# Feed-forward stages with engine orders written by hand, and six inner tiles to a group in place of four

## The chip, the cores and the metric

The kernel runs on one NeuronCore of a Trainium2 chip. The time is device microseconds of one execution, as the runtime measures it; the number given for a kernel is the median of its runs. One execution was also recorded by the hardware profiler, and its span is counted from the first to the last instruction in that record.

Names of engines: PE is TensorE (matmuls), DVE is VectorE, ACT is ScalarE, POOL is GpSimd, SP is SyncE, which here only issues the transfers. PSUM is the memory that PE writes and DVE and ACT read, SBUF the working memory.

## The reference, cut to what matters

One decoder layer on 1024 tokens and 16 meta tokens in front of them (1040 columns in all), width 1024, inner width 2816. It is a feed-forward block, a mixing block with two kinds of attention, and a second feed-forward block:

```
def swiglu(x, w_gate, w_up, w_down):
    return (jax.nn.silu(x @ w_gate) * (x @ w_up)) @ w_down
...
h = h + 0.5 * swiglu(rmsnorm(h, norm_ffn1[l]), w_ffn1_gate[l], w_ffn1_up[l], w_ffn1_down[l])
...
h = h + merged @ w_out[l]
h = h + 0.5 * swiglu(rmsnorm(h, norm_ffn2[l]), w_ffn2_gate[l], w_ffn2_up[l], w_ffn2_down[l])
```

Everything is float32. The change touches the two feed-forward blocks alone; the first works on 1040 columns, the second on 1024.

## The kernel before, in words

**Numbers.** Each float32 operand is split into two float16 parts, a high one (written by ACT) and the rest, a low one (written by DVE, value minus high part). A product is then three matmuls: high by high, high by low, low by high.

**Tiles.** The 2816 inner channels are 22 inner tiles of 128. The columns are two halves (528 and 512 in the first block, 512 and 512 in the second). One *product* is a block of weights by a block of one column half: for a gate or an up projection four contraction tiles times three matmuls, in the first block twice that, since a half goes into two PSUM banks there (S = 2), and once in the second (S = 1).

**Seven products for eight.** Two inner tiles, two halves of the contraction and two halves of the columns make a two by two block product. `fast` does it with seven products in place of eight, named p1, p6, p7, p5, c11, p74 and p53. For that the weights of the pair are combined (`sums`: four additions on DVE), and the columns too (`combine`: four subtractions on POOL, once for the normed input in `make_t`, and once per pair of inner tiles for the hidden values). The products land in PSUM tiles pa, pb, pc and pd; p7 goes into pc, is taken out by DVE, and p74 later adds into the same pc; so p74 waits until DVE has taken p7 out. A set of seven products is called a *job* here: a gate job, an up job, or a down job (two output tiles d and d+1 for all inner tiles of a group).

**Stages of a block.** `plain_pair` does the first pair of inner tiles with eight products while `make_t` builds the combined columns; this is the head. Then pairs follow: an up job of the pair, the split of its hidden values (`split_x`, tile `hid`: three tiles, and four combined ones after POOL), and the gate job of the next pair. After each group of inner tiles (`F_GROUPS`) four down jobs add the group's share to `h`. The last group's down projection is plain: eight tiles d per column half, one PSUM tile `pdn` each.

**Weights.** `load_raw` brings 128x1024 float32 from memory by the SP queue into one of two `wst` buffers; `wide_weights` (gate and up) and `joint_weights` (down) make the split and combined weights of a job from one or two of them.

**Order.** Nothing fixes the order by hand: the tile framework's scheduler interleaves all instructions by its own estimates of time when the kernel is built, and each engine then runs its list in that order, waiting where a semaphore has not come.

Lines that the text speaks of (before): L320 matmuls of a job; L144 to L146 plain matmuls; L129 and L130 high and low part of weights; L325 to L328 sums of weights; L234 and L235 high and low part of `hid`; L282 to L285 `combine`; L386, L391, L393, L397, L401 DVE takes p6, p7, p5, p74, p53 of a gate or up job out of PSUM; L427 gate times up; L434 and L445 the same for a down job; L451 and L453 POOL adds a shared part of a down job to `h`; L503 takes `pdn` out; L218 and L221 norm the columns of the half that is done for the mixing block.

Of the kernel before, what the change touches and what calls it, by code (L numbers as in the profile page):

```python
# [26 lines left out]
TOPK = 256  # L27
NEG = -1e30
# [10 lines left out]
F_GROUPS = ((0, 4), (4, 8), (8, 12), (12, 16), (16, 22))  # L39
# [15 lines left out]
def layer_kernel(ctx: ExitStack, tc: tile.TileContext, xT, gains, wgu1, wd1, win, wvi, wbs, wbw, wout,  # L55
# [139 lines left out]
    def fpage(shape, dt, name):  # L195
        return ph["sb"].tile(shape, dt, tag="fp", name=name, bufs=22)
# [29 lines left out]
    def ffn(u, rb, hs, gi, wgu, wd, other_half, passes, saved):  # L226
# [10 lines left out]
        def new_hid(x):  # L237
            made[0] += 1
            return (fpage if made[0] <= 6 else hp)([P, 2, hs[x][0].shape[1]], F16, "hid")
# [18 lines left out]
        t_blocks, ahead = [], []  # L258

        def plain_pair(f):  # L260
            ws = [load_w(wgu[2 * f + i], 1024, raws.pop(0) if raws else None) for i in range(4)]
            vals = [None] * 4
            for x in range(2):
                if x == 1:
                    ahead.append(wide_weights(wgu[2 * f + 4], wgu[2 * f + 6]))
                    t_blocks.extend(make_t())
# [62 lines left out]

        def wide_weights(src1, src2):  # L330
# [4 lines left out]
            sa = ph["sb"].tile([P, 1024], F32, tag="wS", name="sa", bufs=2)  # L335
            sb = ph["sb"].tile([P, 1024], F32, tag="wS", name="sb", bufs=2)
# [4 lines left out]
            x3 = ph["sb"].tile([P, 2, 1024], F16, tag="ws", name="x3", bufs=2)  # L341
            split_w(x3, sb, 1024)
            x4 = ph["sb"].tile([P, 2, 512], F16, tag="w4", name="x4", bufs=2)
            split_w(x4, r2[:, hi], 512)
            return (x1, 0), (x1, 512), (x2, 0), (x2, 512), (x3, 0), (x3, 512), (x4, 0)

        def joint_weights(src, hn):
            r = load_raw(src, 4 * hn)
            q = [slice(i * hn, (i + 1) * hn) for i in range(4)]
            sa = ph["sb"].tile([P, 1024], F32, tag="wS", name="sa", bufs=2)  # L350
            sums(sa[:, q[2]], sa[:, q[0]], sa[:, q[1]], sa[:, q[3]], r[:, q[0]], r[:, q[1]], r[:, q[3]], r[:, q[2]])
            x1 = wsp_tile()
            split_w(x1, r, 3 * hn)
            x2 = wsp_tile()
            split_w(x2, sa, 4 * hn)
            return (x1, 0), (x1, hn), (x2, 0), (x2, hn), (x2, 2 * hn), (x2, 3 * hn), (x1, 2 * hn)

        def fast(weights, blocks):
            a11, a12, s2, s3, s1, s4, a22 = weights
            b11, b21, b22, t1, t2, t3, t4 = blocks  # L360
            pa, pb = wide("pa"), wide("pb")
            product(pa, *a11, b11, wa, wa, True, True)
            yield "p1", pa[:, :, :wa]
            product(pb, *s2, t2, wa, wa, True, True)
            yield "p6", pb[:, :, :wa]
            pc = wide("pc")
            product(pc, *s3, t3, wb, wb, True, True)
            yield "p7", pc[:, :, :wb]
            pd = wide("pd")
            product(pd, *s1, t1, wb, wb, True, True)  # L370
            yield "p5", pd[:, :, :wb]
            product(pa, *a12, b21, wa, wa, False, True)
            yield "c11", pa[:, :, :wa]
            product(pc, *a22, t4, wa, wa, False, True)
            yield "p74", pc[:, :, :wa]
            product(pd, *s4, b22, wb, wb, False, True)
            yield "p53", pd[:, :, :wb]

        def half_products(f, m, blocks, first, done, weights=None):
            make = fbtmp if m else ftmp  # L380
            for what, ps in fast(weights or wide_weights(wgu[2 * f + m], wgu[2 * f + 2 + m]), blocks):
# [22 lines left out]
        def gate_part(f, blocks, weights=None):  # L404
# [16 lines left out]
            half_products(f, 0, blocks, first, done, weights)  # L421
            return gates

        def up_part(f, blocks, gates):
# [31 lines left out]
        for g_, (f0, f1) in enumerate(F_GROUPS):  # L456
# [4 lines left out]
            for f in range(f0, f1, 2):  # L461
# [5 lines left out]
                if f == 0:  # L467
                    gates = gate_part(2, blocks, ahead.pop())
# [648 lines left out]
```

## Time and profile before

| | |
|---|---|
| runs | 2090.22, 2093.07, 2091.82 us, median 2091.82 |
| span of the profiled execution | 2087.6 us; the median of the runs lies 4.2 us above it |
| PE busy | 1953.8 us, 94% of the span |
| DVE busy | 1622.3 us, 78% |
| ACT, POOL busy | 906.1 us, 420.8 us |
| mean granted TensorE clock | 0.985 of 2.4 GHz |
| moved by DMA | 149.05 MB, mean 71 GB/s |
| first block, head / jobs / plain down | 0 to 111.7 / 111.7 to 648.7 / 648.7 to 716.2 us |
| mixing block | 716.2 to 1426.9 us |
| second block, head / jobs / plain down and end | 1426.9 to 1488.2 / 1488.2 to 2007.7 / 2007.7 to 2087.6 us |

How to read it: a matmul's record has a start that is measured and an end that is modelled, so two matmuls in a row overlap in the record, and 94% does not say that PE was at its peak for 94% of the time. What a matmul costs in a stream is read from start to start. A stretch of PE work is costed by counting its matmuls and multiplying by that step; what is left of the stretch was lost, to waits or to a lower clock.

### The profile page before, as it was taken

Reading aid. Unit: us, or ns where it says so; the run is one execution under the profiler, and the core shown is the slowest. Engines: PE = TensorE matmul, PEld = TensorE weight load, DVE = VectorE, ACT = ScalarE, POOL = GpSimd, SP = SyncE. Lnnn points to the kernel's source line nnn. Section 1 sums busy time; section 2 is a strip of 40 time slices with the busy share of each in tenths; the row PEclk is TensorE's granted clock in tenths of the full one; section 3 lists DMA queues with packets and bytes.
Section 4 is the critical chain, followed back from the end, with each engine's and each line's share of the span. In section 5 each row is a group of like instructions: output and inputs, shape, how many; then the busy total and the mean of one; then the engine's idle time right before and its main releaser. Section 6 shows DMA issues by size and latency. Waiting matters only on the chain.

```text
span 2087.6 us, 32850 instructions
## 1 busy us (share of the span) xinstructions
PE 1953.8 (94%) x13068; PEld 1198.1 (57%) x13068; DVE 1622.3 (78%) x2821; ACT 906.1 (43%) x1572; POOL 420.8 (20%) x329
## 2 busy tenths in 40 slices
PE   5899999989999999999999999998899989999997
PEld 4588887878888556554555654444344434444443
DVE  7978777686865789999999955657978686878755
ACT  4442333333333446589885643434433333332332
POOL 3613232231300123222001000003242231314000
PEclk9999999999999999999999999999999999999998
DMA  4021111111213543322010124241111121211223
GB/s 154 11 62 61 51 52 61 41 62 41 71 54 100 173 153 104 101 67 72 16 62 17 32 82 141 76 167 40 51 51 61 41 62 41 80 41 61 58 73 112
DMA packets 56569, 149.05 MB, mean 71 GB/s; under 512 B 7008, under 2 KB 13152, under 8 KB 56416
## 3 DMA queue, kind: packets, MB, share of 16 engines
q1 hardware_dynamic: 56416, 146.96, 22.0%
q8 instruction: 102, 1.67, 0.3%
q14 instruction: 51, 0.42, 0.1%
HBM read 132.11 MB, written 14.76 MB: 70 GB/s over the span
## 4 chain that ended last, share of the span: by engine, by line
PE 52%; DVE 30%; DMA 5%; issue 5%; ACT 4%; POOL 3%; DVEq 0%; SPq 0%; ACTq 0%; POOLq 0%
PE pc L320 10%; PE pd L320 9%; PE pa L320 8%; DVE wsp L130 5%; PE pb L320 4%; DMA wst<-in_wgu_dram 3%; DVE h L434 2%; PE p_br L914 2%; DVE x L130 2%; DVE hid L235 2%; PE pdn L146 2%; PE pdn L144 2%; PE pdn L145 2%; DVE u L221 2%; DVE sc L706 2%
## 5 line engine op out<-in xcount | busy, mean ns | idle before, releaser
L320 PEld LDWEIGHTS <-wsp 128*128 128x128 f16 x4896 | 480.2, 98 | 268.9 <-issue 33.6
L129 ACT ACTIVATE wsp<-wst 128x1024 f16<-128x1024 f32 (+2 forms) x200 | 185.4, 929 | 358.3 <-PE pc L320 197.5
L320 PEld LDWEIGHTS <-x 128*128 128x128 f16 x2160 | 215.2, 100 | 144.8 <-issue 42.8
L130 DVE SCALAR_TENSOR_TENSOR wsp<-wst,wsp 128x1024 f16<-128x1024 f32 (+2 forms) x200 | 242.2, 1212 | 66.1 <-ACT wsp L129 65.8
L320 PE MATMUL pa<-u,wsp 128*128 128x264 f16 (+1 forms) x1440 | 224.7, 310 | 0.0
L453 POOL TENSOR_TENSOR h<-h,base 128x512 f32<-128x512 f32 x64 | 117.7, 1838 | 219.0 <-DVE h L434 219.0
L146 PEld LDWEIGHTS <-wsp 128*128 128x128 f16 x992 | 97.8, 99 | 99.5 <-issue 12.3
L320 PE MATMUL pc<-tb,x 128*128 128x264 f16 (+1 forms) x720 | 122.9, 329 | 31.5 <-DVE c L391 31.5
L145 PEld LDWEIGHTS <-wsp 128*128 128x128 f16 x992 | 98.1, 99 | 88.2 <-issue 6.4
L144 PEld LDWEIGHTS <-wsp 128*128 128x128 f16 x992 | 98.4, 99 | 86.4 <-issue 4.0
L130 DVE SCALAR_TENSOR_TENSOR wsp<-sa,wsp 128x1024 f16<-128x1024 f32 x72 | 102.4, 1422 | 37.2 <-ACT wsp L129 37.2
L129 ACT ACTIVATE wsp<-sa 128x1024 f16<-128x1024 f32 x72 | 75.7, 1052 | 110.7 <-DVE sa L327 37.9
L320 PE MATMUL pb<-tb,wsp 128*128 128x264 f16 (+1 forms) x720 | 113.6, 311 | 9.2 <-ACT tb L234 5.6
L320 PE MATMUL pc<-tb,wsp 128*128 128x256 f16 (+1 forms) x720 | 114.2, 314 | 0.0
L320 PE MATMUL pd<-u,x 128*128 128x256 f16 (+1 forms) x720 | 111.0, 308 | 0.4
L320 PE MATMUL pd<-tb,x 128*128 128x256 f16 (+1 forms) x720 | 110.7, 308 | 0.0
L320 PE MATMUL pc<-hid,wsp 128*128 128x256 f16 (+2 forms) x576 | 94.4, 309 | 16.1 <-DVE h L434 15.9
L727 ACT ACTIVATE jk<-sc,s5nb 128x784 f16<-128x784 f32 (+2 forms) x93 | 97.8, 1052 | 19.0 <-DVE s5nb L742 15.3
L282 POOL TENSOR_TENSOR t<-g,g 128x512 f32<-128x512 f32 x14 | 22.9, 1634 | 376.6 <-DVE g L427 376.6
L146 PE MATMUL p_gate<-u,wsp 128*128 128x512 f16 x256 | 97.0, 379 | 1.4 <-DVE wsp L130 1.4
L144 PE MATMUL p_gate<-u,wsp 128*128 128x512 f16 x256 | 97.0, 379 | 0.0
L145 PE MATMUL p_gate<-u,wsp 128*128 128x512 f16 x256 | 97.0, 379 | 0.0
(223 smaller groups left out, 3986.3 us busy)
## 6 DMA issues: line engine op xcount, KB each, us to landing
wst<-in_wgu_dram SPq DMA_DIRECT2D x88, 512.0 KB, 3.5
wst<-in_win_dram SPq DMA_DIRECT2D x44, 512.0 KB, 3.5
wst<-in_wd_dram SPq DMA_DIRECT2D x32, 512.0 KB, 3.6
wst<-in_wd_dram SPq DMA_DIRECT2D x32, 384.0 KB, 3.2
wst<-in_wout_dram SPq DMA_DIRECT2D x16, 512.0 KB, 3.8
qscr<-ry SPq DMA_DIRECT2D x20, 256.0 KB, 2.2
q<-qscr SPq DMA_DIRECT2D x20, 256.0 KB, 3.1
wst<-in_wbs_dram SPq DMA_DIRECT2D x16, 256.0 KB, 2.9
```

What stands on the lines that cost most here:

```text
L129: nc.scalar.activation(sp[:, 0, :n], st[:, :n], AF.Copy, scale=WS)
L130: nc.vector.scalar_tensor_tensor(sp[:, 1, :n], st[:, :n], WS, sp[:, 0, :n], op0=ALU.mult, op1=ALU.subtract)
L144: nc.tensor.matmul(ps, w[:, 0, wcols], xt[:, 0, xcols], start=start, stop=False)
L145: nc.tensor.matmul(ps, w[:, 0, wcols], xt[:, 1, xcols], start=False, stop=False)
L146: nc.tensor.matmul(ps, w[:, 1, wcols], xt[:, 0, xcols], start=False, stop=stop)
L221: nc.vector.tensor_sub(u[k][:, 1, s0:s1], t[:, :w], u[k][:, 0, s0:s1])
L235: nc.vector.tensor_sub(dst[:, 1, :], src, dst[:, 0, :])
L320: nc.tensor.matmul(ps[:, s, :n], w[:, a, wc], tiles[k][:, y, s * stride:s * stride + n], start=start and k == 0 and j == 0, stop=stop and ...
L434: nc.vector.scalar_tensor_tensor(hv, ps, DS, hv, op0=ALU.mult, op1=ALU.add)
L453: nc.gpsimd.tensor_add(vb(hs[1][e]), vb(hs[1][e]), va(base)[:, :, :wb])
L706: nc.vector.match_replace(out=raw, in_to_replace=m8, in_values=raw, imm_value=MARK)
L727: nc.scalar.activation(junk[:, :w], sc[b][0], AF.Sign, bias=bias[:, j:j + 1], accum_out=s[:, j:j + 1])
```

## The change

It does the following, and nothing else:

- `F_GROUPS` has three groups of six inner tiles and a last one of four, where it had four of four and a last one of six. The order in which the down weights lie in memory follows it.
- All gate, up and down jobs of a block are listed beforehand (`jobs`). The raw weights of a job are fetched two jobs ahead (`fetch`) and prepared one job ahead (`prepare`), in 13 steps in a fixed order. `joint_weights` is gone: a down job now has two loads and four additions, each over all its inner tiles.
- Behind the matmuls of each product, `pump` writes out a seventh (by the weights that stand in the list) of the job's steps: those of the next job's weights and those that split the hidden values of the pair before. Then come the instructions that take the product out of PSUM.
- All this stands in a `manual_schedule` region for PE, DVE, ACT and POOL: on these four engines the order is that of the text. SP's order is still the scheduler's. The head (`plain_pair`) and the plain down projection stand outside.
- A down job does its products in the order p1, p7, p5, p6, c11, p74, p53, and one addition of POOL moves from p5 to p6.
- Buffers: 27 pages `fp` in place of 22; the hidden values of a group take up to 11 of these, 8 of `hp` and 2 of `nt`.

```diff
-F_GROUPS = ((0, 4), (4, 8), (8, 12), (12, 16), (16, 22))
+F_GROUPS = ((0, 6), (6, 12), (12, 18), (18, 22))
...
+        def fetch(i):
+            if i < len(jobs):
+                n = 2 * jobs[i][3]
+                fetched[i] = [load_raw(src, n) for src in jobs[i][1:3]]
...
+        def prepare(i):
...
+            r1, r2 = fetched.pop(i)
...
+            one, two = n / 750, n / 420
+            v = nc.vector
+            return [
+                (0, lambda: high(x1, r1, both)),
+                (one, lambda: v.tensor_add(sb[:, lo], r2[:, lo], r2[:, hi])),
+                (0, lambda: high(x4, r2[:, hi], n)),
+                (one, lambda: v.tensor_sub(sa[:, lo], sb[:, lo], r1[:, lo])),
+                (one, lambda: v.tensor_sub(sa[:, hi], r1[:, lo], r2[:, lo])),
+                (0, lambda: high(x2, sa, both)),
+                (one, lambda: v.tensor_sub(sb[:, hi], r1[:, hi], sa[:, lo])),
+                (two, lambda: low(x1, r1, both)),
+                (one, lambda: low(x4, r2[:, hi], n)),
+                (0, lambda: fetch(i + 1)),
+                (0, lambda: high(x3, sb, both)),
+                (two, lambda: low(x2, sa, both)),
+                (two, lambda: low(x3, sb, both)),
+            ]
...
+        def pump(t):
+            while todo and t > 0:
+                cost, step = todo.pop(0)
+                step()
+                t -= cost
...
+            share = sum(c for c, _ in todo) / len(order)
+            for name in order:
+                bank, w, tiles, stride, n, start = what[name]
+                if bank not in banks:
+                    banks[bank] = wide(bank)
+                ps = banks[bank]
+                product(ps, *w, tiles, stride, n, start, True)
+                pump(share)
+                yield name, ps[:, :, :n]
+            drain()
+
+        UP = ("p1", "p6", "p7", "p5", "c11", "p74", "p53")
+        DOWN = ("p1", "p7", "p5", "p6", "c11", "p74", "p53")
...
+            own = prepare(i + 1)
+            todo.extend(own[:7] + tail[:4] + own[7:10] + tail[4:] + own[10:])
...
+        vals = plain_pair(0)
+        blocks = (u[0][:4], u[0][4:], u[1][4:]) + tuple(t_blocks)
+        with tc.manual_schedule(engines=ORDERED):
+            for f0, f1 in F_GROUPS:
...
+                    if last:
+                        extra = []
+                        split_later(extra, vals[1], 1)
+                        hid += [[down[0][-1], extra[0]], [down[1][-1], down[2][-1]]]
+                        if f == NF - 2:
+                            drain()
...
+                if not last:
+                    for d in range(0, KD, 2):
+                        fast_down(d, down)
```

How the change moves instructions on DVE, at two places. First the passage from an up job to the gate job after it, in the first block: from the last product of the up job (gate times up, `g`) to where the gate job's p7 is taken out (`c<-pc,base`, L391 before, L458 now); `sa` and `sb` are sums of weights, `base<-pb` is p6 taken out, `hid<-t` and the `hid` rows behind it are splits of what POOL has combined. Before:

```order
L427 SCALAR_TENSOR_TENSOR g_1409<-base,g_1409 128x512
L130 SCALAR_TENSOR_TENSOR x_2317<-sb,x_2317 128x1024
L325 TENSOR_TENSOR sb<-wst 128x512
L235 TENSOR_TENSOR hid<-t_2075,hid 128x512
L235 TENSOR_TENSOR hid<-g_1355,hid 128x528
L235 TENSOR_TENSOR hid<-g_1409,hid 128x512
L235 TENSOR_TENSOR hid<-c_1381,hid 128x528
L386 TENSOR_TENSOR base<-pb,base 128x528
L326 TENSOR_TENSOR sa<-sb,wst 128x512
L327 TENSOR_TENSOR sa<-wst 128x512
L328 TENSOR_TENSOR sb<-wst,sa 128x512
L391 TENSOR_TENSOR c_2192<-pc,base 128x512
```

The same passage as it is now:

```order
L494 SCALAR_TENSOR_TENSOR g_995<-base,g_995 128x512
L541 TENSOR_TENSOR hid<-g_940,hid 128x528
L541 TENSOR_TENSOR hid<-c_967,hid 128x528
L541 TENSOR_TENSOR hid<-c_875,hid 128x512
L390 TENSOR_TENSOR sb<-wst 128x512
L392 TENSOR_TENSOR sa<-sb,wst 128x512
L393 TENSOR_TENSOR sa<-wst 128x512
L453 TENSOR_TENSOR base<-pb,base 128x528
L395 TENSOR_TENSOR sb<-wst,sa 128x512
L541 TENSOR_TENSOR hid<-t_1207,hid 128x512
L541 TENSOR_TENSOR hid<-g_995,hid 128x512
L458 TENSOR_TENSOR c_1317<-pc,base 128x512
```

All four splits of combined values stood ahead of p6 and p7; now two stand between them and two behind p7, and the three plain splits, which before were done inside the up job, stand at the front.

Second the end of the last up job and the beginning of the plain down projection, in the first block (`c<-pc`, `base<-pd`: p74 and p53 taken out; `h<-pdn`: the first plain tile taken out). Before:

```order
L427 SCALAR_TENSOR_TENSOR g_6655<-pa,g_6655 128x528
L130 SCALAR_TENSOR_TENSOR wsp<-wst,wsp 128x768
L235 TENSOR_TENSOR hid<-g_6655,hid 128x528
L397 TENSOR_TENSOR c_6889<-pc,base 128x528
L427 SCALAR_TENSOR_TENSOR c_6681<-c_6889,c_6681 128x528
L235 TENSOR_TENSOR hid<-c_6681,hid 128x528
L235 TENSOR_TENSOR hid<-c_6602,hid 128x512
L401 TENSOR_TENSOR base<-pd,base 128x2x256
L427 SCALAR_TENSOR_TENSOR g_6709<-base,g_6709 128x512
L235 TENSOR_TENSOR hid<-g_6709,hid 128x512
L503 SCALAR_TENSOR_TENSOR h<-pdn,h 128x528
```

The same place now:

```order
L494 SCALAR_TENSOR_TENSOR g_6857<-pa,g_6857 128x528
L131 SCALAR_TENSOR_TENSOR wsp<-wst,wsp 128x512
L464 TENSOR_TENSOR c_7069<-pc,base 128x528
L494 SCALAR_TENSOR_TENSOR c_6883<-c_7069,c_6883 128x528
L468 TENSOR_TENSOR base<-pd,base 128x2x256
L494 SCALAR_TENSOR_TENSOR g_6911<-base,g_6911 128x512
L541 TENSOR_TENSOR hid<-g_6857,hid 128x528
L541 TENSOR_TENSOR hid<-c_6883,hid 128x528
L541 TENSOR_TENSOR hid<-c_6800,hid 128x512
L541 TENSOR_TENSOR hid<-g_6911,hid 128x512
L588 SCALAR_TENSOR_TENSOR h<-pdn,h 128x528
```

All four splits of the last pair now stand behind the last product's two instructions; before, three of them stood ahead of it.

On PE the products of the head and of the mixing block stand in the same order as before, and so does DVE's list from the first rotary product of the mixing block on.

## Rows read from the trace of the kernel before

**Rows 1.** The page, part 1: busy time, share of the span, instructions of each engine.

```profile
PE 1953.8 (94%) x13068; PEld 1198.1 (57%) x13068; DVE 1622.3 (78%) x2821; ACT 906.1 (43%) x1572; POOL 420.8 (20%) x329
```

**Rows 2.** Stretches: length, busy time and (count) of PE, PEld, DVE, ACT, POOL, clock, DMA.

```profile
111.70:648.70 537.00, 514.26 (x4562) 448.06 (x4561) 401.51 (x537) 176.16 (x244) 125.19 (x76) 0.99 0.18 55
1488.20:2007.70 519.50, 499.05 (x2280) 224.08 (x2280) 396.16 (x539) 178.39 (x247) 126.13 (x76) 0.99 0.18 57
```

**Rows 3.** The chain that ended last, by time: start us, us, what; undisturbed products.

```profile
114.62 2.70 PE pa L320 x24
...
122.64 2.62 PE pd L320 x24
...
1609.90 2.59 PE pa L320 x12
```

**Rows 4.** Whom PE waited for in the first block's jobs: total us, times, longest.

```profile
PE pc L320 <- DVE c L391: 13.1, 7, 3.8
PE pc L320 <- DVE h L434: 9.3, 8, 1.6
```

**Rows 5.** The same view, the second block's jobs.

```profile
PE pc L320 <- DVE c L391: 13.7, 5, 4.0
PE pc L320 <- DVE h L434: 6.6, 5, 1.6
```

**Rows 6.** Timeline of PE, one gate job: start us, us, what, [idle before <-releaser].

```profile
221.65 2.86 PE L320 MATMUL pa<-u,wsp 128*128 128x264 f16 x24
228.34 4.37 PE L320 MATMUL pc<-tb,x 128*128 128x264 f16 x24 [3.83 <-DVE c L391]
```

**Rows 7.** Timeline of DVE from the up job into that gate job.

```profile
205.92 1.22 DVE L130 SCALAR_TENSOR_TENSOR wsp<-wst,wsp 128x1024 f16<-128x1024 f32 x1
207.06 0.68 DVE L328 TENSOR_TENSOR sb<-wst,sa 128x512 f32<-128x512 f32 x1
207.66 0.68 DVE L393 TENSOR_TENSOR c<-pd,c 128x512 f32<-128x512 f32 x1
...
218.43 0.87 DVE L325 TENSOR_TENSOR sb<-wst 128x512 f32<-128x512 f32 x1 [0.81 <-DMA wst<-in_wgu_dram]
219.45 1.53 DVE L235 TENSOR_TENSOR hid<-t,hid 128x512 f16<-128x512 f32 x1
222.81 1.84 DVE L235 TENSOR_TENSOR hid<-g,hid 128x528 f16<-128x528 f32 x2 [1.83 <-ACT hid L234]
```

**Rows 8.** Timeline of ACT, the copy that DVE waited for there.

```profile
222.14 1.16 ACT L234 ACTIVATE hid<-g 128x528 f16<-128x528 f32 x2 [2.22 <-POOL g L284]
```

**Rows 9.** The stretch around it, columns as in Rows 2.

```profile
203.00:236.00 33.00, 28.83 (x244) 24.28 (x242) 26.78 (x39) 12.19 (x18) 6.69 (x4) 0.95 0.16 49
```

**Rows 10.** Timeline of POOL there, two of the four instructions of `combine`.

```profile
218.83 1.60 POOL L283 TENSOR_TENSOR g<-c,g 128x512 f32<-128x512 f32 x1
...
222.18 1.30 POOL L285 TENSOR_TENSOR c<-c,g 128x528 f32<-128x528 f32 x1
```

**Rows 11.** POOL's costliest group in the first block's jobs: count, busy us, mean ns, idle before.

```profile
L453 POOL TENSOR_TENSOR h<-h,base 128x512 f32<-128x512 f32 x32 | 58.8, 1839 | 114.6 <-DVE h L434 114.6
```

**Rows 12.** The page, part 6: loads of gate and up weights, KB each, us to landing.

```profile
wst<-in_wgu_dram SPq DMA_DIRECT2D x88, 512.0 KB, 3.5
```

**Rows 13.** Timeline of DVE in the plain down projection, first block.

```profile
661.91 0.96 DVE L130 SCALAR_TENSOR_TENSOR wsp<-wst,wsp 128x768 f16<-128x768 f32 x1 [0.17 <-ACT wsp L129]
662.79 0.70 DVE L160 TENSOR_TENSOR acc<-acc,sq 128x528 f32<-128x528 f32 x1
```

**Rows 14.** DVE's groups from 690 to 730 us: count, busy us, mean ns, idle before.

```profile
L218 DVE SCALAR_TENSOR_TENSOR un<-h,g_all,nbc 128x272 f32<-128x272 f32 (+1 forms) x16 | 7.2, 483 | 0.0
L221 DVE TENSOR_TENSOR u<-un,u 128x272 f16<-128x272 f32 (+1 forms) x16 | 6.6, 428 | 0.3
```

**Rows 15.** Who waited for the tile pdn, first block: us, times.

```profile
PE rp L144: 1.8, 1
```

**Rows 16.** Timeline of PE in the first block's head.

```profile
92.59 0.39 PE L320 MATMUL pb<-tb,wsp 128*128 128x264 f16 x2 [3.06 <-ACT tb L234]
```

More of the change, by code (lines that the diff above doesn't have):

```diff
@@ L264, in plain_pair @@
                 if x == 1:
-                    ahead.append(wide_weights(wgu[2 * f + 4], wgu[2 * f + 6]))
+                    weights[0] = wide_weights(*jobs[0][1:3])
+                    fetch(1)
                     t_blocks.extend(make_t())
@@ L340, in wide_weights @@
             split_w(x2, sa, 1024)
[L341 removed]
+            x3, x4 = late_tiles()
             split_w(x3, sb, 1024)
[L343 removed]
             split_w(x4, r2[:, hi], 512)
[L345 to L356, printed above, removed]
@@ L364, in fast @@
[L364 to L375, printed above, removed]
@@ L376, in fast @@
-            product(pd, *s4, b22, wb, wb, False, True)
-            yield "p53", pd[:, :, :wb]
-        def half_products(f, m, blocks, first, done, weights=None):
+            what = {"p1": ("pa", a11, b11, wa, wa, True), "p6": ("pb", s2, t2, wa, wa, True),
+                    "p7": ("pc", s3, t3, wb, wb, True), "p5": ("pd", s1, t1, wb, wb, True),
+                    "c11": ("pa", a12, b21, wa, wa, False), "p74": ("pc", a22, t4, wa, wa, False),
+                    "p53": ("pd", s4, b22, wb, wb, False)}
@@ L380, in half_products, with joint @@
+        DOWN = ("p1", "p7", "p5", "p6", "c11", "p74", "p53")
+        turn = [0]
+        def joint(blocks, order):
+            i = turn[0]
+            turn[0] += 1
+            own = prepare(i + 1)
+            todo.extend(own[:7] + tail[:4] + own[7:10] + tail[4:] + own[10:])
+            tail.clear()
+            return fast(weights.pop(i), blocks, order)
+        def half_products(m, blocks, first, done):
             make = fbtmp if m else ftmp
-            for what, ps in fast(weights or wide_weights(wgu[2 * f + m], wgu[2 * f + 2 + m]), blocks):
+            for what, ps in joint(blocks, UP):
@@ L419, in done, with up_part @@
                     gates[i] = (t, v)
-            half_products(f, 0, blocks, first, done, weights)
+            half_products(0, blocks, first, done)
             return gates
-        def up_part(f, blocks, gates):
+        def up_part(blocks, gates):
             def done(i, v):
@@ new lines, in ffn @@
+        ready = None
+        for x, subs, done in passes:
+            c0, c1 = subs[0][0], subs[-1][1]
+            full = c1 - c0 == hs[x][0].shape[1]
+            acc = new_acc()
+            for d in range(KD):
+                nd = (f1 - f0) * P
+                w = load_w(wd[d // 2][:, 2 * f0 * P + d % 2 * nd:2 * f0 * P + (d % 2 + 1) * nd], nd)
+                ps = wide("pdn")
+                if full:
+                    plain(ps, w, [t[x] for t in hid], x)
+                    pv, hv = pview(ps, x), tview(hs[x][d], x)
+                else:
+                    pv, hv = ps[:, 0, :c1 - c0], hs[x][d][:, c0:c1]
+                    proj(pv, w, [t[x] for t in hid], c0, c1)
+                nc.vector.scalar_tensor_tensor(hv, pv, DS, hv, op0=ALU.mult, op1=ALU.add)
+                square_into(d, hs[x][d][:, c0:c1], acc[:, c0:])
+                if d == 0:
+                    warm = small(1, "n_warm")
+                    nc.scalar.activation(warm, acc[:, c0:c0 + 1], AF.Sqrt)
+                if ready and d == 0:
+                    r = norm_stats(*ready[:2])
+                if ready and d == 1:
+                    ready[2](r)
+            ready = acc, subs, done
```

151 lines of the change are left out of this document (79 added, 72 removed).

## The prediction

> **What bounds the kernel now.** I first read the page's busy shares: PE is busy for 94% of the span, with DVE next at 78% [rows 1]. The time is therefore set by PE, and the question is how far PE is from its own undisturbed step. For that I read products in which nothing interferes, from start to start: 24 matmuls of 264 columns in 2.70 us (0.1125 each), 24 of 256 in 2.62 (0.109), 12 of 512 in 2.59 (0.216) [rows 3]. A job of the first block has four products of the first kind and three of the second, on average 0.1111 us a matmul. Then I read the stretches that hold the jobs [rows 2]. First block: 4562 matmuls x 0.1111 = 506.8 us, in 537.0: **30.2 us lost**. Second block: 2280 x 0.2158 = 492.0, in 519.5: **27.5 us lost**.
>
> Where these go, the view of waits says: PE stands for pc or the other banks until DVE has taken a product out, 13.1 and 9.3 us in the first block, 13.7 and 6.6 in the second [rows 4, 5]. That is 42.7 of 57.7. The rest I put down to two things seen in one gate job [rows 6]. The wait shows as 3.83 us, yet p74 behind it took 4.37 instead of 2.70, since it ran in part at the lower clock: the stretch around it has a granted clock of 0.95 [rows 9]. And a wait is shown short, since the matmul before it has a modelled end.
>
> Why DVE is late there is in its timeline [rows 7]. It is not short of time: it stands idle for 1.83 us just then. It stands in front of `hid<-g`, which needs ACT's copy [rows 8], which needs POOL's combination. The instruction that takes p7 out stands behind it in the list, and it is the one that PE waits for until 228.34 [rows 6]. So what is lost is the order of DVE's list.
>
> **The change, part by part.**
>
> *The order in the gate jobs.* Two of the four combined splits now stand ahead of p7 and two behind, and the three plain ones stand at the front. I add up what DVE does from the gate job's start to p7's removal. A 512-column instruction takes 0.60 us from start to start (207.06 to 207.66) and a low part of 1024 columns 1.14 (205.92 to 207.06) [rows 7]. Ahead of p7 come a carry-over of two (1.2), three splits (1.8), three sums (1.8), p6 (0.6), a sum (0.6), two splits (1.2): 7.2 us, and p7 itself 0.6.
>
> POOL comes on top. A split that began at 219.45 took 1.53 in place of 0.68 [rows 7]: POOL was at an instruction that ended at 220.43 [rows 10], and the split ended at 220.98, one step of its own behind. So it stood until POOL was done. POOL's instruction alone takes 1.30 [rows 10]; the longer ones have a DVE instruction inside them. The two take turns, and four of POOL's cost DVE up to 5.2 us: p7 is out at 7.8 + 5.2 = 13.0. p74 wants pc after five products, 5 x 2.67 = 13.3 us. So the wait goes, with 0.3 us in hand; with half the turns, as where DVE reads PSUM or waits, 2.9. I take no wait, and a sixth of a microsecond in each of 18 gate jobs for those that miss it, **+3**.
>
> The Trainium skill, page "SBUF — State Buffer", section "SBUF: two separate sides", has the rule for this: DVE and GpSimd share a port pair under an exclusive lock, and a DVE instruction with two SBUF inputs is held for the whole of a GpSimd instruction that reads SBUF. Rows 7 and 10 agree with it to 0.1 us. By a plain doubling of the one split, without the rule, p7 would be out near 9 us, and the 3 us would not be in the sum.
>
> *DVE's load per job*, since a fixed list helps nothing if it does not fit. Gate job: four sums 2.4, three low parts 3.4 and a half one 0.6, five removals 3.0, seven splits 4.2: 13.6 of PE's 18.7 us. Up job: 11.8, with four products by the gate in place of the splits. Down job of six tiles: six removals 3.6, four sums of 384 (0.47 each, between nothing and 0.60) 1.9, low parts of 768 columns three times 0.88 [rows 13] and a half one 0.5: 8.6 of 14.0, to which POOL's three additions bring up to 3.9. All fit. ACT is busy for a third of these stretches [rows 2] and has the same copies as before: I cost it at nothing. I take **-30.2 and -27.5**.
>
> *The weights.* A load of 512 KB lands in 3.5 us [rows 12]. The loads of the job after next are issued behind a job's last reader of the raw weights, some 10 to 12 us into a gate job and 7 into a down job by the steps ahead of them; 7 us remain in either case. SP's queue is not moved past anything: in these stretches it carries weights alone. Cost nothing; if a load took over 7 us, DVE's sums would wait for it, and removals behind them.
>
> *Groups of six.* Down jobs: before 16 of 7 x 12 matmuls, 16 x 9.33 = 149.3 us; now 12 of 7 x 18, 12 x 14.0 = 168.0: +18.7. The plain down projection of eight d and two halves falls from six tiles to four: in the first half 36 matmuls become 24, 4.05 to 2.70 us, in the second 18 become 12, 3.89 to 2.59; eight times both, 63.5 to 42.3: -21.2. Net **-2.5**. In the second block -20.7 and +18.1, net **-2.6**. POOL has four jobs' additions fewer in each block, three of up to 1.8 us each [rows 11], off the path.
>
> *The end of the hand-ordered stretch.* All four splits of the last pair now stand behind p53's two instructions. PE can do the old pair's six matmuls meanwhile, 0.67 us in the first block, 1.3 in the second. The first new split is done three DVE steps and an ACT copy after p53, some 2.1 us. That leaves a hole of **+1.4** and **+0.7**; before, three of these splits stood ahead of p53.
>
> *The shorter plain passes.* In the second pass of the first block PE needs 8 x 2.59 = 20.7 us. DVE needs eight removals and eight low parts of 512 columns (9.6) and the norm of the first half, 13.8 us busy in 32 instructions [rows 14], some 11.2 from start to start: 20.8. Before, it was 23.0 against 31.1, a cover of 8 us that is now gone. What is late next is the last `pdn`, and the first rotary product, which already waited 1.8 us for it [rows 15], with a weight split of 1.14 behind. Between nothing and 3, I take **+1.5**.
>
> *The head* loses one low part of 1024 columns from among the splits that PE waits for there, 3.06 us once in the first block [rows 16]. Between nothing and all of it in either block, I take **-1** for the two together. *Six passages between groups* have a new mixture of job kinds, which the trace does not show; half a DVE step each, **+2**.
>
> Sum: -30.2 - 27.5 - 2.5 - 2.6 + 1.4 + 0.7 + 1.5 - 1 + 2 + 3 = -55.2. From the span of 2087.6 that is 2032.4; the median of the runs lies 4.2 above that execution's span, so **2036.6 us**.
>
> **Rivals.**
>
> 1. *POOL and DVE in turns do not fit.* If POOL's instructions cost DVE their whole 6.7 us [rows 9], p7 is out at 14.5, and p74 waits 1.2 us. In 18 gate jobs that is 21 us in place of the 3, with a lower clock behind a few of them up to 24, and 8 where only a third of the jobs miss: **2042 to 2058**. For it: the margin is 0.3 us, and the carry-over of two is an estimate. Against it: the 6.7 hold DVE's own instructions, which would be counted twice.
>
> 2. *The waits move rather than go.* The removal of another product (p6, or a down job's first) stands behind a step that is not ready, and half of the loss stays: 57.7 / 2 is 29 back, and up to all but a few: 2058 to 2085. Against it: nothing in the new list ahead of a removal needs POOL's result of the same product.
>
> 3. *Slower than before: weights arrive late.* The place is the first sum of each job's preparation, with the removals of p6 and p7 behind it on DVE. Now each load is issued in the middle of the job before the one in which it is read. It begins to cost when landing takes more than 7 us, twice the row's 3.5. PE then loses what is over that, less the 0.3 in hand. To eat up the gain of 55, each of 62 jobs has to lose 0.9 us: landing at 7 + 0.3 + 0.9 = 8.2 us, 2.3 times the row. For it: a sum did wait 0.81 us for a load before [rows 7]. Against it: the DMA share is 0.18 in these stretches [rows 2]. The time would be **2095 to 2110**.
>
> 4. *The change does not do what it says.* The rows of the order show that it does; the time would be the old one.
>
> **How the numbers follow.** The forecast, 2022 to 2042, gets 0.70: the low end has the heads' waits gone too (3 each), no slips (5) and no loss at the handover (3.6), the high one 3 us at the passage to the mixing block and twice the slips. Rival 1 gets 0.18, rival 2 0.05, rival 3 0.05, rival 4 0.02. The range 2022 to 2058 holds the forecast, of which I leave a little for outside, and rival 1: somewhat over 8 in 10. A measurement of this kernel can tell 0.2% from no change, about 4 us: forecast and rivals 1 and 2 are faster by more (0.93), rival 4 the same (0.02), rival 3 slower (0.05).
>
> **What would show it.** Right: in the job stretches PE's waits for DVE's removal of p7 and for the down jobs' sums are gone, the stretch is its count of matmuls times 0.1111 or 0.2158 to within 3 us, the granted clock there is 1.00, and holes of 1 to 2 us stand at the last pair's splits. p7's removal begins 10 to 13 us after a gate job's p1. Wrong: the wait for pc is there again in most gate jobs with POOL at work beside DVE (rival 1), PE waits for another bank (rival 2), DVE's sums stand idle for a load (rival 3), or the jobs keep their time per matmul while the plain passes do not shrink by 21 us each.

## The result, and the profile after

| | before | after |
|---|---|---|
| runs, median | 2092.21 us (2090.22 to 2093.07, 4 runs) | 2033.12 us (2031.50 to 2034.67, 4 runs) |
| ratio, 95% interval | | 0.9713, 0.9700 to 0.9727 |
| span of the profiled execution | 2087.6 us | 2031.1 us |

The change takes 56.5 us off the span; forecast were 55.2. By the medians it takes off 59.1: the span of the kernel before lies 4.6 us under the median of its runs, that of the kernel after 2.0. The page's first part has PE at 95% in place of 94 [rows 1], which tells little. The stretches tell more. Of the kernel after, in the order jobs of the first block, plain down projection, the beginning of the mixing block, jobs of the second block, plain down projection to the end; columns are length, then busy time and (count) of PE, PEld, DVE, ACT and POOL, granted clock, DMA share, GB/s:

```profile
114.80:637.28 522.48, 522.48 (x4707) 460.28 (x4704) 404.10 (x512) 175.13 (x256) 110.12 (x68) 1.00 0.18 56
637.28:685.78 48.50, 44.90 (x311) 30.31 (x308) 41.07 (x81) 24.33 (x46) 0.95 (x1) 0.99 0.57 185
685.78:712.00 26.22, 26.22 (x169) 17.70 (x170) 16.13 (x30) 10.67 (x18) 6.88 (x9) 0.89 0.52 163
...
1463.09:1971.72 508.63, 508.44 (x2353) 230.10 (x2352) 402.80 (x513) 174.28 (x257) 109.48 (x68) 1.00 0.19 58
1971.72:2031.10 59.38, 46.49 (x225) 23.27 (x223) 43.62 (x76) 20.09 (x35) 0.00 (x0) 0.90 0.35 115
```

The same places of the kernel before, cut at the same products (the rows shown ahead of the prediction begin 3 us earlier, still in the first job of the block):

```profile
114.45:648.69 534.24, 511.50 (x4539) 445.63 (x4537) 399.81 (x535) 176.16 (x244) 125.19 (x76) 0.99 0.18 55
648.69:716.24 67.55, 65.78 (x454) 44.55 (x452) 48.68 (x88) 30.28 (x52) 0.95 (x1) 1.00 0.55 171
1490.80:2007.73 516.93, 496.49 (x2269) 222.90 (x2268) 394.41 (x537) 176.36 (x244) 126.13 (x76) 0.99 0.18 56
2007.73:2087.60 79.87, 67.37 (x321) 32.98 (x319) 46.44 (x75) 22.01 (x35) 0.00 (x0) 0.92 0.32 102
```

```profile
716.24:742.00 25.76, 25.76 (x195) 18.59 (x195) 13.97 (x26) 7.70 (x14) 8.25 (x10) 1.00 0.47 148
```

In the first block's jobs PE is now busy for 522.48 of 522.48 us at a granted clock of 1.00: 19 jobs of 18.66 and 12 down jobs of 14.0 make 522.5, so nothing is lost. In the second block 19 x 18.13 + 12 x 13.6 = 507.6, in 508.63: 1.0 us lost. By PE's starts it lies in five gate jobs, 0.2 us in each: there p74 could begin 12.95 us behind p1, when c11 is done, and p7's removal ends at 13.1. In neither stretch does the view of waits, which leaves out the shortest, list a wait of PE; the rows of before had 42.7 us there [rows 4, 5]. What is left of PE's waits for products lies in the first job of each block, where p74's wait for p7's removal has grown, from 2.5 and 2.1 us to 3.6 and 2.8; and the wait ahead of the mixing block has grown too [rows 15]:

```profile
PE pc L327 <- DVE c L458: 6.4, 2, 3.6
...
PE rp L145 <- DVE un L219: 3.5, 1, 3.5
```

One gate job of the kernel after, by PE's timeline (columns as in [rows 6]):

```profile
133.46 2.86 PE L327 MATMUL pa<-u,wsp 128*128 128x264 f16 x24
136.16 2.86 PE L327 MATMUL pb<-tb,wsp 128*128 128x264 f16 x24
138.86 2.78 PE L327 MATMUL pc<-tb,wsp 128*128 128x256 f16 x24
141.48 2.78 PE L327 MATMUL pd<-tb,x 128*128 128x256 f16 x24
144.10 2.86 PE L327 MATMUL pa<-u,wsp 128*128 128x264 f16 x24
146.80 2.86 PE L327 MATMUL pc<-tb,x 128*128 128x264 f16 x24
```

and DVE and POOL beside it, to be held against [rows 7] and [rows 10]:

```profile
133.66 0.69 DVE L468 TENSOR_TENSOR base<-pd,base 128x512 f32<-128x512 f32 x1 [1.17 <-PE pd L327]
...
135.61 3.45 DVE L541 TENSOR_TENSOR hid<-c,hid 128x528 f16<-128x528 f32 x2
138.99 1.75 DVE L390 TENSOR_TENSOR sb<-wst 128x512 f32<-128x512 f32 x1
140.78 1.68 DVE L392 TENSOR_TENSOR sa<-sb,wst 128x512 f32<-128x512 f32 x1
142.37 0.68 DVE L393 TENSOR_TENSOR sa<-wst 128x512 f32<-128x512 f32 x1
142.97 0.70 DVE L453 TENSOR_TENSOR base<-pb,base 128x528 f32<-128x528 f32 x1
143.59 0.68 DVE L395 TENSOR_TENSOR sb<-wst,sa 128x512 f32<-128x512 f32 x1
144.69 0.69 DVE L541 TENSOR_TENSOR hid<-t,hid 128x512 f16<-128x512 f32 x1 [0.43 <-ACT hid L540]
145.30 0.68 DVE L541 TENSOR_TENSOR hid<-g,hid 128x512 f16<-128x512 f32 x1
145.90 0.68 DVE L458 TENSOR_TENSOR c<-pc,base 128x512 f32<-128x512 f32 x1
```

```profile
135.22 1.60 POOL L289 TENSOR_TENSOR t<-g,g 128x512 f32<-128x512 f32 x1 [32.90 <-DVE g L494]
136.90 1.62 POOL L290 TENSOR_TENSOR g<-c,g 128x512 f32<-128x512 f32 x1
138.48 1.71 POOL L291 TENSOR_TENSOR g<-c,t 128x512 f32<-128x512 f32 x1
140.27 1.63 POOL L292 TENSOR_TENSOR c<-c,g 128x528 f32<-128x528 f32 x1
```

Two rows of the kernel before, of the gate job that began at 211.0:

```profile
214.60 0.69 DVE L401 TENSOR_TENSOR base<-pd,base 128x512 f32<-128x512 f32 x1
216.64 2.12 POOL L282 TENSOR_TENSOR t<-g,g 128x512 f32<-128x512 f32 x1 [18.30 <-DVE g L427]
```

PE goes from product to product with no gap. DVE takes the up job's last product out 0.2 us into the gate job (before, 3.6 us in), and POOL begins 1.8 us in (before, 5.6). From 135.6 DVE gets one instruction in per instruction of POOL: two splits take 3.45 us, two sums 1.75 and 1.68, and the next, with POOL done, 0.68. p7's removal ends at 146.58, 13.1 us behind p1; p74 starts at 146.80.

### The profile page after: what moved, and what is told of

The parts are those of the page before. It is cut to its first block, busy times and chain, and to the rows that moved or that the text cites. A ratio compares the mean times of both kernels' runs of the same rounds, so it can differ in the third digit from the quotient of the medians.

```text
span 2031.1 us, 32839 instructions
## 1 busy us (share of the span) xinstructions
PE 1936.5 (95%) x13080; PEld 1197.3 (59%) x13080; DVE 1627.2 (80%) x2779; ACT 901.0 (44%) x1602; POOL 386.9 (19%) x313
## 4 chain that ended last, share of the span: by engine, by line
PE 70%; DVE 18%; ACT 4%; issue 4%; DMA 2%; POOL 2%; DVEq 0%; SPq 0%; ACTq 0%; POOLq 0%
PE pc L327 14%; PE pd L327 14%; PE pa L327 14%; PE pb L327 7%; PE p_br L999 2%; DVE sc L791 2%; DVE u L222 2%; DVE wsp L131 1%; PE p_gate L147 1%; PE p_gate L145 1%; PE p_gate L146 1%; DVE m L790 1%; PE p_out L146 1%; PE p_out L147 1%; PE p_out L145 1%
## 5 line engine op out<-in xcount | busy, mean ns | idle before, releaser
L327 PEld LDWEIGHTS <-wsp 128*128 128x128 f16 x4176 | 410.0, 98 | 214.2 <-issue 12.3
L327 PEld LDWEIGHTS <-x 128*128 128x128 f16 x3132 | 307.3, 98 | 157.9 <-issue 8.5
L131 DVE SCALAR_TENSOR_TENSOR wsp<-wst,wsp 128x1024 f16<-128x1024 f32 (+2 forms) x130 | 134.8, 1038 | 54.6 <-ACT wsp L130 54.3
L130 ACT ACTIVATE wsp<-wst 128x1024 f16<-128x1024 f32 (+2 forms) x130 | 111.7, 863 | 140.1 <-PE p_out L147 45.9
L147 PEld LDWEIGHTS <-wsp 128*128 128x128 f16 x912 | 90.5, 99 | 94.5 <-issue 12.3
L145 PEld LDWEIGHTS <-wsp 128*128 128x128 f16 x912 | 91.0, 100 | 85.1 <-issue 4.1
L146 PEld LDWEIGHTS <-wsp 128*128 128x128 f16 x912 | 90.7, 99 | 80.2 <-issue 3.9
L327 PE MATMUL pc<-tb,x 128*128 128x264 f16 (+1 forms) x720 | 113.9, 313 | 6.6 <-DVE c L458 6.4
L341 ACT ACTIVATE wsp<-sa 128x1024 f16<-128x1024 f32 (+1 forms) x62 | 60.2, 971 | 103.4 <-DVE sa L393 103.4
L327 PE MATMUL pa<-hid,wsp 128*128 128x264 f16 (+1 forms) x648 | 103.1, 310 | 0.0
L341 ACT ACTIVATE wsp<-wst 128x1024 f16<-128x1024 f32 (+1 forms) x62 | 59.9, 967 | 94.3 <-DMA wst<-in_wgu_dram 49.9
L327 PE MATMUL pd<-hid,x 128*128 128x256 f16 (+1 forms) x648 | 101.6, 308 | 0.0
```

The costliest lines, as they stand in the source:

```text
L130: nc.scalar.activation(sp[:, 0, :n], st[:, :n], AF.Copy, scale=WS)
L131: nc.vector.scalar_tensor_tensor(sp[:, 1, :n], st[:, :n], WS, sp[:, 0, :n], op0=ALU.mult, op1=ALU.subtract)
L145: nc.tensor.matmul(ps, w[:, 0, wcols], xt[:, 0, xcols], start=start, stop=False)
L146: nc.tensor.matmul(ps, w[:, 0, wcols], xt[:, 1, xcols], start=False, stop=False)
L147: nc.tensor.matmul(ps, w[:, 1, wcols], xt[:, 0, xcols], start=False, stop=stop)
L327: nc.tensor.matmul(ps[:, s, :n], w[:, a, wc], tiles[k][:, y, s * stride:s * stride + n], start=start and k == 0 and j == 0, stop=stop and ...
```

## Experiments

The runs fall into three questions. All times are medians; the kernel before was measured with each batch, at 2091.0, 2092.5 and 2090.8 us.

### Is it the order, the groups, or the rest?

**Without the region.** The four engines are left to the scheduler, all else stays.

```diff
-        with tc.manual_schedule(engines=ORDERED):
+        if True:
```

> The region in which the order is that of the text is taken away; groups, jobs, loads and the dealt-out steps stay, and the framework's scheduler orders all engines by its own estimates again. Theory (the order is what gives the time): the waits of PE for the removals of p7 and of the down jobs' products return, most of 57 us, 2075 to 2095 us. Rival (two jobs of lead for the loads and the groups are enough, in any order): 2033 to 2045 us.

2047.25 us (2043.67 to 2050.41), ratio 0.9785, 0.9771 to 0.9798. Between both: the fixed order itself is worth 14 us, not 57. The waits of p74 in the gate jobs are back (first block, then second; one of the fourteen is in an up job), those in the down jobs are not:

```profile
PE pc L327 <- DVE c L458: 5.7, 5, 1.5
```

```profile
PE pc L327 <- DVE c L458: 7.4, 9, 2.4
```

**Old groups, order by hand.**

```diff
-F_GROUPS = ((0, 6), (6, 12), (12, 18), (18, 22))
+F_GROUPS = ((0, 4), (4, 8), (8, 12), (12, 16), (16, 22))
```

> The hand-written orders stay, the groups of inner tiles go back to 4, 4, 4, 4, 6. Theory (the order by hand gives the 57 us, the groups only their matmuls, and the short plain passes lose cover at the handover to the mixing block): +2.5 and +2.6 us of matmuls, -4.5 us at the handover (the first rotary product waits about 1.9 us in place of 3.7, and the clock does not fall behind it), 2034 us, within 3. Rival (a down job of four tiles is too short for DVE and POOL in turns: 7.1 us of DVE and 3.9 of POOL against 9.3 of PE): up to 1.7 us lost in each of 32 down jobs, 2040 to 2088 us.

2033.51 us (2032.48 to 2034.14), ratio 0.9719. As the theory had it: with the order by hand the groups of six bring nothing, since the 5 us of matmuls that they save go again at the handover (with the old groups the first rotary product waits 1.5 us and the matmuls behind it run at the upper clock: 4.8 us less than in the change).

**Old groups, scheduler's order.** Both edits above.

> As in the run without the region, and the groups are 4, 4, 4, 4, 6 again. Theory (longer down jobs relieve DVE and POOL, and with the scheduler's order this counts): the waits in down jobs come back, some 1.8 us in ten or so of 32, with one of 4 us in the gate job behind some groups: 2060 to 2085 us. Rival (the lead of one job for the weights and two for the loads is what took the waits away): 2047 us, within 4.

2060.35 us (2054.71 to 2061.96), ratio 0.9843. The theory's side, at its low end: under the scheduler groups of six are worth 13 us. In the second block p74 waits again in down jobs (h) and in gate and up jobs (c; the three waits of over 1 us are in gate jobs):

```profile
PE pc L327 <- DVE c L458: 8.9, 7, 2.4
PE pc L327 <- DVE h L501: 4.2, 4, 1.6
```

**The order of a down job's products.** First under the scheduler (with groups of six), then by hand:

```diff
-        DOWN = ("p1", "p7", "p5", "p6", "c11", "p74", "p53")
+        DOWN = UP
```

> As in the run without the region (order again by the scheduler), and a down job does its products in the order of the other jobs, p6 ahead of p7, as before the change. Some 42 of the 57 us were kept there without the order by hand; this and the next run ask by which part. Theory (down jobs of six tiles are long enough that any order fits): 2047 us, within 4. Rival (p7 early is what took away the waits of p74 for the removal of p7 in down jobs, 9.3 and 6.6 us before): 2059 to 2066 us.

> Order by hand, groups of six, but in a down job p6 stands ahead of p7 as before the change. p74 follows p7 by three products in place of four, still 6 us. Theory (no wait in sight): 2033 us, within 3. Rival (the new order of the products is needed): p74 waits about 1 us in each of 24 down jobs, 2050 to 2060 us.

2048.17 us (2046.24 to 2049.16) and 2034.71 us (2032.20 to 2036.94). No difference in either: with groups of six this part of the change is worth nothing that the runs can tell. With groups of four it was not tried.

**The lead of the weights**, under the scheduler and with old groups: a job's weights are prepared in its own text, ahead of its products. The `drain()` writes out all steps there, the splits too, so that nothing is dealt out over the products either.

```diff
-            own = prepare(i + 1)
+            own = prepare(i) if i else []
...
             tail.clear()
+            drain()
```

> Scheduler's order and old groups, and a job's weights are prepared in the text of the job itself, ahead of its products, and not in the job before; their loads stand one job ahead and not two. Theory (lead): the waits of before come back, 1.8 us in the down jobs and 4 with a half clock behind the groups: 2080 to 2095 us. Rival (the scheduler hoists the weights by itself, and the new form of the down weights, two loads and four additions over all tiles, took the 32): 2060 us, within 5.

2061.32 us (2057.53 to 2062.98): the theory falls, the lead is worth nothing under the scheduler, which hoists the weights by itself (the first sum for the up job that begins at 229.87 us runs at 213.76). The run shows more than that. With old groups, no region, no lead and no dealing some 30 of the 57 us are there. By PE's starts the jobs behind the first lose 30.0 us in place of 57.8: the down jobs 7.3 for 19.1, the gate and up jobs 22.7 for 38.7.

**The dealing out**, under the scheduler and with old groups: all steps stand behind p1.

```diff
-                pump(share)
+                drain()
```

> Scheduler's order and old groups (2060 us, of which 32 us less than before are unexplained), and the steps of the next job's weights and of the splits are no longer dealt out over the products in the text, but all stand behind p1. Theory (the lead of the weights took the 32 us, the dealing in the text is undone by the scheduler): 2060 us, within 5. Rival (the place in the text is the scheduler's guide, and the dealing took the 32): 2080 to 2095 us.

2075.80 us (2073.46 to 2076.37), ratio 0.9924. Neither theory: where the steps stand in the text guides the scheduler by 15 us. It is not the dealing as such, since the run before this one, with all steps ahead of the job, has the time of the dealt-out kernel; what seems to cost is their place behind p1.

### What bounds the order by hand?

**Not dealt out**, the same edit with the region and groups of six.

> Order by hand and groups of six as in the change, but the steps are not dealt out: all of them stand behind p1 on DVE, ahead of every removal. Same instructions, same engines. Theory (it is the place of the removals in DVE's list that counts): in a gate job p7's removal ends 1.2 + 4.2 + 2.4 + 4.0 + 5.2 (POOL's turns) + 1.2 = 18.2 us behind p1, p74 waits 4.9 us in 16 gate jobs and the clock falls behind it, 80 to 105 us more: 2113 to 2140 us, slower than the kernel before. Rival (DVE has 4 us a job to spare, and a hand-fixed order of any kind does): 2033 to 2045 us.

2134.94 us (2133.58 to 2135.53), ratio 1.0208, 1.0194 to 1.0222: slower than the kernel before, with the same instructions on the same engines as the change. The theory's number, and its mechanism with one link more. Of PE's waits that it adds:

```profile
PE pa L327 <- ACT base L451: 66.4, 18, 7.4
...
PE pc L327 <- DVE c L458: 6.8, 8, 2.1
```

PE, ACT and DVE in one gate job:

```profile
153.49 4.26 PE L327 MATMUL pa<-u,wsp 128*128 128x264 f16 x24 [3.48 <-ACT base L451]
158.45 2.86 PE L327 MATMUL pc<-tb,x 128*128 128x264 f16 x24 [0.70 <-DVE c L458]
```

```profile
148.84 1.06 ACT L341 ACTIVATE wsp<-sa 128x1024 f16<-128x1024 f32 x1 [7.93 <-DVE sa L393]
...
152.85 0.59 ACT L451 ACTIVATE base<-pa 128x528 f32<-128x528 f32 x1
```

```profile
157.71 0.69 DVE L458 TENSOR_TENSOR c<-pc,base 128x512 f32<-128x512 f32 x1
```

The job's p1 is at 139.21. c11 waits first, for ACT's copy of p1 (`base<-pa`), which stands on ACT behind the high parts of sums that DVE has not made yet: ACT stands idle for 7.93 us ahead of them. Then c11 runs in part at the lower clock (4.26 in place of 2.86 in the record), and then p74 waits for DVE. p74 starts 19.2 us behind p1 in place of 13.3. The waits for ACT are ten times those for DVE, but they do not stand in place of them: on the way to p7's removal DVE waits 1.0 us for ACT's copy of a split and never for c11; the removal ends at 158.40, 19.2 us behind p1, and would have held p74 until then by itself. So ACT's list, which I had costed at nothing, is as much a part of the order as DVE's.

**All four combined splits ahead of the sums.**

```diff
-            todo.extend(own[:7] + tail[:4] + own[7:10] + tail[4:] + own[10:])
+            todo.extend(tail + own)
```

> All four combined splits of a pair are put ahead of the weight sums, so that on DVE they all stand ahead of p7's removal, as they did before the change. Theory (DVE was late before because its whole list ran some 3 us behind and POOL's combination began late with it; POOL and DVE take turns): DVE waits now in time that POOL uses anyway, p7 is out some 11 us after a gate job's p1 instead of 13.1, no wait of p74, time 2032 us, within 3 of the changed kernel. Rival (what cost the time before was that the splits stand ahead of p7): p74 waits 2 to 4 us in 16 gate jobs, 2065 to 2095 us.

2033.68 us (2033.36 to 2036.62), ratio 0.9723. The view of waits lists none in the jobs behind the first; p7's removal ends 12.8 us behind p1, not 11, and 0.6 ahead of p74. As the steps are dealt out by weight, two of the sums now stand behind p7's removal, and the list up to it is as long as in the change. So it isn't the place of the splits by itself that cost the time before.

**One more instruction of POOL** per pair.

```diff
             nc.gpsimd.tensor_sub(va(a2), va(a2), va(a1))
+            if more:
+                nc.gpsimd.tensor_sub(idle, vb(b2), vb(t1))
```

> POOL does one more subtraction of 128x512 behind each pair's combination, into a tile that nobody reads (18 instructions in all, 16 of them in gate jobs with little in hand; no other engine gets anything to do or to wait for). Theory (POOL and DVE take turns, and 0.05 to 0.8 us are in hand): DVE is held 1.3 us longer ahead of p7's removal, p74 waits about 1.1 us in ten of these jobs and 0.6 in six, some 15 us: 2048 us, 2042 to 2056. Rival (they only slow each other where they meet, and the 0.05 us in hand is chance): 2033 us, within 3.

2051.21 us (2048.41 to 2051.85), ratio 0.9799. An engine that is 19% busy, with a result that nobody reads, makes the kernel 18 us slower. The sum `sa` took 0.68 us above at this place; here it is held:

```profile
144.02 1.78 DVE L396 TENSOR_TENSOR sa<-wst 128x512 f32<-128x512 f32 x1
```

```profile
143.51 1.74 POOL L295 TENSOR_TENSOR idle<-c,t 128x512 f32<-128x512 f32 x1
```

```profile
149.39 2.86 PE L330 MATMUL pc<-tb,x 128*128 128x264 f16 x24 [0.78 <-DVE c L461]
```

By starts PE loses 0.92 to 0.95 us here and in four more jobs of the first block, 0.31 in three, 1.27 to 1.30 in five of the second and 0.67 to 0.70 in three: 14.1 us in all, 1.0 of which the change loses too; some 15 were expected (1.1 in ten jobs, 0.6 in six). The first jobs of both blocks, in which the first pair is combined, are together 3.3 us longer, which was not expected. The Trainium skill's rule of the exclusive lock (page "SBUF — State Buffer", section "SBUF: two separate sides") agrees with this: the held instruction ends 0.55 us behind POOL's (145.80 to 145.25).

### The handover to the mixing block

**Six tiles last, in the first block alone.**

```diff
+F_GROUPS1 = ((0, 6), (6, 12), (12, 16), (16, 22))
...
+        groups = F_GROUPS1 if gi == 0 else F_GROUPS
```

> In the first block alone the groups are 6, 6, 4, 6, so that its plain down projection has six tiles again; the order by hand stays. Theory (the short plain pass leaves DVE no cover for the norm of the first half): +2.5 us of matmuls, the wait of the first rotary product falls from 3.7 to under 2 us and the granted clock over the 31 us from there rises from 0.89 to 1.00, together -4.5: 2031 us. Rival (the wait there has nothing to do with the plain pass's length): 2035.5 us.

2032.73 us (2030.40 to 2035.36), ratio 0.9717, span 2028.9. The span of the profiled execution is 2.2 us shorter (2.0 were worked out), but the spans of this kernel's runs alone lie 4.9 us apart, so neither spans nor times can tell it from the change. The mechanism shows: the first rotary product's wait and the stretch behind it,

```profile
PE rp L146 <- DVE h L590: 1.8, 1, 1.8
```

```profile
684.93:711.00 26.07, 26.07 (x199) 18.92 (x199) 14.33 (x29) 7.70 (x14) 8.51 (x11) 1.00 0.50 152
```

have 1.8 us and a clock of 1.00 again.

**Both harmless edits**, this one and the splits ahead of the sums.

> The two edits that did no harm together: groups 6, 6, 4, 6 in the first block, and the combined splits ahead of the sums. Theory (the first takes 2.2 us off the span, the second 0.3): span 2028.5 us, time 2031 us, within 3; at the edge of what the runs can tell from the change. Rival (in groups of four the splits ahead of the sums make p7's removal late again): 2036 to 2045 us.

2028.94 us (2027.06 to 2030.72, 5 runs), ratio 0.9700, 0.9686 to 0.9713; the span is 2028.9. This is the fastest kernel of the study, and its five runs lie below the four of the change. But its interval overlaps that of the change (0.9700 to 0.9727), and the two were not timed in one batch; that it is better is likely and not shown.

## Why the prediction came out

| term | forecast | measured | from |
|---|---|---|---|
| jobs, first block | -30.2 | -30.3 | 534.24 less 503.9 of matmuls, to 522.48 less 522.5 |
| jobs, second block | -27.5 | -26.5 | 516.93 less 489.4, to 508.63 less 507.6 |
| fewer matmuls | -5.1 | -5.1 | by their count |
| holes at the region's end | +2.1 | +0.4 | PE's starts behind the last p53 |
| handover to the mixing block | +1.5 | +4.5 | wait 1.8 to 3.5, and 2.8 behind it |
| the heads and first jobs | -1 | +0.9 | PE's starts |
| slips in gate jobs and passages | +5 | in the jobs | 0.0 and 1.0 us of theirs |
| the rest of the plain passes, the mixing block and the end | 0 | -0.4 | PE's starts |
| sum | -55.2 | -56.5 | |

The time itself was put at 2036.6 us and is 2033.1: 1.3 of the 3.5 us are the sum's, and 2.2 come from the 4.2 between the span and the median before, which I carried over; after the change it is 2.0.

**The stretches' losses** went in full but for 1.0 us, and by the mechanism of DVE's load: in the first block p7's removal was put at 13.0 us behind p1 with 0.3 in hand, and ends at 13.1 with 0.2. The reading that POOL and DVE take turns carried this; with it, the waits that one more POOL instruction makes could be forecast to a microsecond, the time of that run to three (2048 for 2051.2). That the 13.0 is met so closely is luck: POOL's four instructions cost DVE some 4.3 us and not 5.2 (135.61 to 142.37, less four steps of its own), while the carry-over is 1.5 and not 1.2, and ahead of `hid<-t` DVE is idle for ACT's copy, 0.5 us from start to start, which I had not counted. And the 13.3 at which p74 wants pc holds for the first block alone; in the second it is 5 x 2.59 = 12.95, and there was nothing in hand.

**"What is lost is the order of DVE's list"** is the step that holds only in part. The place that I named, the combined splits ahead of p7, is not what cost the time: with all four ahead of it and the list up to it no longer than now, nothing waits. What differs from before is that DVE was already 3.6 us late at the end of the up job, and POOL with it (5.6 us into the gate job in place of 1.8). The loss was lateness in in-order lists, and the fixed order removes it; but other parts remove much of it in other ways. In steps: 2091 before, 2076 with the new jobs and weights but all steps behind p1, old groups and the scheduler's order, 2060 with the steps dealt out (or all ahead of the job, 2061), 2047 with groups of six as well, 2033 with the order fixed. They overlap: the groups are worth 13 us under the scheduler and nothing by hand, the dealing, against all steps behind p1, 15 and 102. So no single one "gives" the 57. Where the first 30 come from, at 2061, is not settled: that kernel differs from the one before in the form of the down weights (two loads, four additions over all tiles), in the buffers, in the order of a down job's products and in where the steps stand in the text. The last two were tried with other parts in place, not by themselves; the form and the buffers were not tried.

**The end of the region** was mis-sized: I counted six matmuls that PE could do. It did 18 before the first wait, of 0.27 us: the plain projection is outside the region, and matmuls that need none of the late splits have been put ahead of those that do.

**The handover** was mis-sized the other way. The wait itself was right (+1.7 for +1.5), and so was its ground, that DVE's norm has lost its cover: the first rotary product now waits for the norm (`un`), where before it waited for the last `pdn` to be taken out. (DVE's list there is not quite the old one, as it was said to be: two `acc` additions and a weight split now stand behind the first rotary product's removal.) I left out what comes behind it:

```profile
685.78 0.39 PE L145 MATMUL rp<-u,wsp 128*128 128x272 f16 x1 [3.50 <-DVE un L219]
...
691.17 0.43 PE L145 MATMUL rp<-u,wsp 128*128 128x272 f16 x1
691.40 0.33 PE L146 MATMUL rp<-u,wsp 128*128 128x272 f16 x1
691.56 0.28 PE L147 MATMUL rp<-u,wsp 128*128 128x272 f16 x1
691.68 0.28 PE L145 MATMUL rp<-u,wsp 128*128 128x272 f16 x1
```

From 685.78 to 691.40 a matmul of 272 columns steps by 0.227 us, behind it by 0.116: the lower and the upper level of the clock. That is half of 5.6 us, 2.8. The wait of 1.8 us at this place before was followed by no such stretch; in the run without the region a wait of 3.4 us was, of half the length, with 1.3 us lost by the same count. The same was in [rows 6], behind the hole of 3.83 us, and I had used it for the losses that go but not for the hole that grows.

**The heads** and first jobs were to lose 1 us and are 0.9 us longer. The wait for ACT in the first block, which was to shrink, is not smaller (3.3 us for 3.1). p74's grown waits in the first jobs, which I had not looked at, make these 0.3 and 0.1 us longer; 0.5 us lies ahead of the first job of the second block, and its cause stays open.

**The slips** (+5) came to 0.0 and 1.0 us. The slips and the holes were put 5.7 us too high, the handover and the heads 4.9 too low; that these errors nearly cancel is luck. The ends of the forecast are added up a microsecond off: their own terms give 2023.0 and 2043.1 for 2022 and 2042.

**The rivals:** turns that do not fit missed by 0.2 us in the first block and came about in small in the second, 0.2 us in five gate jobs where 1.2 in 18 were feared; the run with one more POOL instruction is this rival in full. Waits that move: the view of waits lists none in the jobs behind the first. Late weights: in neither stretch of jobs does the view of waits show DVE waiting for a load.

## What to carry to other kernels

Where an engine is in order and has time to spare, look for what stands ahead of the instruction that another engine waits for, sum that list to it, and compare with the time at which it is wanted; add what GpSimd's instructions hold DVE for where both work on SBUF (here 1.1 us for each of 128x512). Do the same for the other engines' lists: in the worst order here ACT's copy was late as well. A fixed order is worth what the list in it is worth: here the same instructions gave 2033 and 2135 us. A hole that grows (here from 1.8 to 3.5 us) can cost more behind it, in clock, than by itself.

## What the hardware showed that was not expected

That an engine at 19% load, with a result that nobody reads, can cost the kernel a microsecond for each instruction. And the turns are strict: POOL's four instructions in the gate job above hold DVE four times, and each of these instructions of DVE (the two in 3.45 us, 1.75, 1.68) ends 0.54 to 0.56 us behind one of POOL's. An instruction of DVE that reads PSUM is not held: 25 removals in the trace of the kernel after overlap an instruction of POOL by more than 0.25 us, and none takes over 0.71. In a down job of the kernel after, DVE's removal of a product and the addition of POOL in the midst of which it stands:

```profile
241.67 0.70 DVE L501 SCALAR_TENSOR_TENSOR h<-pa,h 128x528 f32<-128x528 f32 x1
```

```profile
240.70 2.19 POOL L512 TENSOR_TENSOR h<-h,base 128x512 f32<-128x512 f32 x1 [6.66 <-DVE base L511]
```

It takes the 0.70 us that it takes alone, while the addition goes on to 242.89. So here the removals from PSUM are the part of DVE's list that POOL does not lengthen.
